# Expert weights loaded in rows of 8 KB through 16 ring places instead of rows of 4 KB through 32

## The chip, the cores and the metric

The kernel runs on one core of one Trainium2 chip. Its time is the device time of one execution in microseconds (us). Before the change the median of three runs was 1579.39 us (1577.28 to 1581.19). A separate execution was recorded by the hardware profiler; it took 1578.24 us, and its span, from the first to the last instruction, was 1576.4 us. The names of the engines are those of the profile: PE (matrix products), PEld (its weight loads), DVE, ACT, POOL, SP. SP's instructions here are almost only DMA issues; 16 DMA engines do the transfers.

## The reference

One layer of a decoder trunk over 512 tokens of width 1024, all in float32:

```python
u   = x @ w_in                                  # (512, 1024) @ (1024, D_IN_PROJ)
mix = concat[SSD(u_a), RWKV7(u_b), GLA(u_c), mLSTM(u_d)] @ w_out
x   = LayerNorm(DEEPNORM_ALPHA * x + mix)
h   = DEEPNORM_ALPHA * x + MoE(x)               # top 4 of 32 experts
h   = h + sigmoid(h @ ple_gate_w) * (p @ ple_proj)
x   = LayerNorm(h)

# MoE: for each token its 4 experts by router logits, gate = softmax of the 4
hg, hl = split(x @ w_gu[e] + b_gu[e])           # w_gu[e]: 1024 x 2048
hg, hl = min(hg, 7), clip(hl, -7, 7)
y      = ((hl + 1) * hg * sigmoid(1.702 * hg)) @ w_down[e] + b_down[e]   # w_down[e]: 1024 x 1024
```

RWKV7 is a recurrence over the tokens with a 64 x 64 state for each of 4 heads; the kernel computes it in blocks of tokens, one block after the other. The expert weights are 32 x 12 MB, by far most of what is read.

## The kernel before

The work has four stages. In the first, the four mixers are computed; in the second, the product with `w_out`, the first LayerNorm and the router, which ranks the experts and writes lists of each expert's tokens. The third is the MoE, the fourth the gate product with `ple_gate_w` and the second LayerNorm.

An expert's 12 MB are read as 24 units of 512 KB, each a tile of 128 partitions x 1024 floats, so that a row of a unit, what one partition receives, is 4 KB. Units 0 to 15 hold the gate and up weights (line 1297, tile `gu`), units 16 to 23 the down weights (line 1308, tile `dn`). The host stores the weights in this layout. The tokens of an expert are gathered from `x1d` by POOL (line 1208, `xg`), transposed by PE (line 1279, `tr`) and then multiplied in groups: 18 of the experts take three groups and 14 take two, 82 groups in all. Every group walks through the whole expert's weights, as four products of 128x512 for each 1024 rows of `gu`.

The units pass through a ring of places in SBUF, used in the fixed order `seq`. The places belong to pools that serve the mixers or the tail at other times:

```python
seq = ["rb"] * 7 + ["r2"] * RING2 + ["rb"] * (SLOTS["rb"] - 9) + ["wr"] * 2 + ["r3"] * RING3 + ["rb"] * 2
```

That is 32 places of 4 KB a partition, and four more (`pp`) that are used in the first round alone. `ahead` (line 898) issues 15 units while the out-projection runs (`"pf": {(0,1):15}`); the rest is issued by `unit`, for the first two experts from fixed addresses (line 1231), for the others from an address that SP reads from the router's result (line 1229). A place is given to a new unit when `used` has been called for the old one:

```python
if old is not None and not kept[old]:
    return False
w = R["raw"]()
...
sy.dma_start(w[:, None], A["we"][bass.ds(place[j], 1), u].rearrange("o p n -> p o n"))
```

The order of the instructions of one engine is set when the kernel is built, by a list scheduler that takes the next ready instruction by its own estimate of times; in the MoE PE's order is held to the order of the code. On the chip each engine runs its list in order, and a wait holds up all that stands behind it. SP's DMA loads wait for the place to be free and, as there are eight completion counters on its queue, for the load eight before it.

In the mixers, the 14 `rb` places hold RWKV's tiles: `sgw`, `aa`, `gg`, `rk`, `rr`, `kp` (elementwise inputs), `AR`, `KB` and `G` (operands and Gram blocks), `Lx` (the blocks to be inverted), `AQ` and `Tt` (the inverse and its pieces). The chain is: `G` products, a solve on DVE, `Q` and `Z` products (PE, `AQ`), then the sequential steps with `U<-W,Tt`, transposes `oT`, and `y_rwkvh`, `y_rwkvl`, which the out-projection (`mix`) reads. In between PE has the other mixers' input projections (`pj`, `pt`).

Of the kernel before, what the change touches and what calls it, by code (L numbers as in the profile page):

```python
# [8 lines left out]
F32 = mybir.dt.float32  # L9
# [11 lines left out]
D = 1024  # L21
E = 32
# [1 line left out]
KT = 8  # L24
C0 = math.exp(-0.5)

SLOTS = {"rb": 14, "xh": 8, "wr": 2, "wh": 2, "wl": 2, "zb": 4, "zc": 7, "yy": 2, "rc": 4, "rd": 6, "mc": 5, "md": 4}
BANKS = {"r": 2, "o": 1, "p": 2, "m": 3}
RING2 = 8
RING3, XG, AB = 8, 2, 2  # L30
NS = 3


BIG = 18
TURN = [0, 1] + sorted(range(2, 32), key=lambda r: (r - 1.5) / (BIG - 2) if r < BIG else (r - BIG + 0.7) / (32 - BIG))
GROUPS_OF = [NS if r < BIG else NS - 1 for r in range(32)]
OPT = {"conv": ("sx0",), "lnt": ("vv","va","aa","va"), "lov": ("zb",), "pl": (0,5,8,13,16,21), "pt": (), "em": 20, "wk": 6, "ml": 0, "hold": 0, "gm": (0,), "pe": 0, "order": "SABZDIgvLqmoM", "wm": (10,8,0), "bn": (), "ad": (), "rb": (2,0,3), "pf": {(0,1):15}, "ex": 4, "xq": 1, "aq": 1,  "ap": 2, "t1": (8,8), "pa": 1,  "op": ((2,1),(0,))}
EMPTY = 4096.0


# [86 lines left out]
def mixers(tc, nc, A, rbp, dram, mix, ctx, ident, ones, tri, x1d, accd, R, dbg):  # L127
# [153 lines left out]
    def rwkv():  # L281
# [103 lines left out]
        td = [dram.tile([2, 2, 32, 512], F32, name=f"td{n}") for n in range(2)]  # L385
        for t_, src in zip(td, (Tx, Tn)):
            sy.dma_start(t_.rearrange("q d b n -> (q d b) n"), flat(src))
        AQ = tl("rb", [128, 32, 32], "AQ")
        Tt = [tl("rb", [128, 16, 64], f"Tt{n}") for n in range(2)]
        for q in range(2):  # L390
            sy.dma_start(AQ[64 + 16 * q:80 + 16 * q], td[0][q, 0].rearrange("b (t u) -> t b u", u=32))
# [481 lines left out]
    def wout(h, kq, *tags):  # L873
        return split(A["wO"][h, kq], [128, 2, 512], "wo", *tags)

    seq = ["rb"] * 7 + ["r2"] * RING2 + ["rb"] * (SLOTS["rb"] - 9) + ["wr"] * 2 + ["r3"] * RING3 + ["rb"] * 2

    room = {**SLOTS, "r2": RING2, "r3": RING3, "pp": NT}

    def raw(look=False):  # L880

        n = R["n"]
        if n < len(seq) + OPT["ex"]:
            tag = (seq[:-2] + ["pp"] * OPT["ex"] + seq[-2:])[n]
        else:
            tag = seq[(n - OPT["ex"]) % len(seq)]
        if look:
            return tag, R["at"].get(tag, 0) % room[tag]
        R["n"] += 1
        R["at"][tag] = R["at"].get(tag, 0) + 1  # L890
        return R["pools"][tag].tile([128, D], F32, name="w", tag=tag, bufs=room[tag])

    def ahead(n):

        for _ in range(n):
            R["taken"].append(raw(look=True))
# [162 lines left out]
def moe(ctx, tc, nc, A, ident, rbp, R, x1d, accd, ovt, ove, out, dbg):  # L1059
# [64 lines left out]
    def gateweights():  # L1124

        for k in range(KT):
            w = ring[len(srcs) - KT + k]
            pool, tag, n = [(R["pools"]["r3"], "r3", RING3), (R["pools"]["wr"], "wr", SLOTS["wr"])][k] if k < 2 else (rbp, "rb", SLOTS["rb"])
            hi, lo = (pool.tile([128, D], F32R, name=x, tag=tag, bufs=n) for x in ("wh", "wl"))
            s.activation(hi, w, AF.Copy)  # L1130
            v.tensor_sub(lo, w, hi.bitcast(F32))
            wg.append((hi, lo))


    def ordered(m):
# [79 lines left out]
    def unit(tag_of, src):  # L1215

        if R["pre"]:
            ring.append(R["pre"].pop(0))
            return True
        tag, n = R["peek"]()  # L1220
        old = waits.get((tag, n))
# [3 lines that stand above are left out]
        if isinstance(src, tuple):  # L1225
            j, u = src
            if j not in place:
                place[j] = nc.values_load(eii[0:1, TURN[j]:TURN[j] + 1], engines=[mybir.EngineType.SP], min_val=0, max_val=E - 1)
            sy.dma_start(w[:, None], A["we"][bass.ds(place[j], 1), u].rearrange("o p n -> p o n"))
        else:  # L1230
            sy.dma_start(w, src)
        waits[tag, n] = len(ring)
        ring.append(w)
        return True

    srcs = []
    for e in range(E):
        if e == OPT["em"]:
            srcs += [A["pT"], A["pproj"][0], A["pproj"][1]]
        srcs += [A["we"][e, u] if e < 2 else (e, u) for u in range(24)]  # L1240
    srcs += [A["pgw"][k] for k in range(KT)]
    base = lambda e: 24 * e + (3 if e >= OPT["em"] else 0)
# [50 lines left out]
    def up(p, e, xT, g_, ks, last):  # L1293
        for k in ks:
            for c in range(4):
                w = ring[base(e) + 2 * k + c // 2][:, 512 * (c % 2):512 * (c % 2) + 512]
                ordered(pe.matmul(p[32 * c:32 * c + 32], xT[:, k, g_:32 * GROUPS_OF[TURN[e]]:GROUPS_OF[TURN[e]]], w,  # L1297
                                  start=False, stop=(k == KT - 1), tile_position=(0, 32 * c)))
            if last:
                used(base(e) + 2 * k)  # L1300
                used(base(e) + 2 * k + 1)

    def down(p, e, hT, ks, last):
        m = None
        for k in ks:
            for c in range(4):
                w = ring[base(e) + 16 + k][:, 256 * c:256 * c + 256]
                m = ordered(pe.matmul(p[32 * c:32 * c + 32, 0:256], hT[:, k % 2, 32 * (k // 2):32 * (k // 2) + 32], w,  # L1308
                                      start=False, stop=(k == KT - 1), tile_position=(0, 32 * c)))
            if last:  # L1310
                used(base(e) + 16 + k)
        return m

    def swiglu(p):
# [30 lines left out]

    def embed(i, tag):

        at = base(OPT["em"]) - 3
        pT, *pw = ring[at:at + 3]
        ppt.append(tp.tile([128, D], F32, name=f"pp{i}", tag="pp", bufs=NT))  # L1350
        tk = slice(128 * i, 128 * i + 128)
        for h in range(2):
            p = bank(tag, "emb")
            n = slice(512 * h, 512 * h + 512)
            for k in range(2):
                ordered(pe.matmul(p, pT[:, 512 * k:512 * k + 512][:, tk], pw[k][:, n], start=(k == 0), stop=(k == 1)))
            s.activation(ppt[i][:, n], p, AF.Copy)
        if i == NT - 1:
            for i in range(3):
                used(at + i)  # L1360

    def blocks():
# [35 lines left out]
    def overflow(then):  # L1398
        with tc.tile_pool(name="ov", bufs=1) as ov:
            n = nc.values_load(tot[0:1, 0:1], min_val=0, max_val=24)  # L1400
            with tc.For_i(0, n, 1) as j:
# [23 lines left out]
                v.scalar_tensor_tensor(gi_, d[:, 0:1], EMPTY, d[:, 1:2], op0=ALU.add, op1=ALU.add)  # L1425
                v.tensor_add(d[:, 3:4], d[:, 2:3], d[:, 3:4])
                v.tensor_add(d[:, 3:4], d[:, 3:4], d[:, 4:5])
                def big(name):
                    return ring2.tile([128, D], F32, name=name, tag="r2", bufs=RING2)

                x = big("x")
                g.memset(x, 0.0)
# [193 lines left out]
def _lay_out(inp, experts=True):  # L1626
# [77 lines left out]
```

## Time and profile before

| | |
|---|---|
| median of 3 runs | 1579.39 us (1577.28 to 1581.19) |
| profiled execution | 1578.24 us, span 1576.4 us |
| PE busy | 1462.9 us (93%) |
| PEld, DVE, ACT, POOL busy | 776.0, 522.9, 301.7, 218.2 us |
| DMA | 466.13 MB, 296 GB/s over the span |

The first `gu` product starts 404.64 us after the span's start. A product's busy time includes waits inside PE's pipeline, since the ends of products are modelled; so PE busy at 93% does not say that PE works at its peak for 93% of the span. In the rows below a window gives a stretch in us from the start of the span; the DMA share is that of 16 engines (it can be a little over 1, as the packets of several queues on one engine overlap in the record).

### The profile page before, as it was taken

Reading aid. Unit: us, or ns where it says so; the run is one execution under the profiler, and the core shown is the slowest. Engines: PE = TensorE matmul, PEld = TensorE weight load, DVE = VectorE, ACT = ScalarE, POOL = GpSimd, SP = SyncE. Lnnn points to the kernel's source line nnn. Section 1 sums busy time; section 2 is a strip of 40 time slices with the busy share of each in tenths; the row PEclk is TensorE's granted clock in tenths of the full one; section 3 lists DMA queues with packets and bytes.
Section 4 is the critical chain, followed back from the end, with each engine's and each line's share of the span. In section 5 each row is a group of like instructions: output and inputs, shape, how many; then the busy total and the mean of one; then the engine's idle time right before and its main releaser. Section 6 shows DMA issues by size and latency. Waiting matters only on the chain. (4 is left out here: it accounts for less than half of the span.)

```text
span 1576.4 us, 36036 instructions
## 1 busy us (share of the span) xinstructions
PE 1462.9 (93%) x14672; PEld 776.0 (49%) x14672; DVE 522.9 (33%) x1597; ACT 301.7 (19%) x632; POOL 218.2 (14%) x222
## 2 busy tenths in 40 slices
PE   9989999997799999999999999999999998999985
PEld 5769879886244433443334333334434343334364
DVE  5688875668521112111121111111121111111155
ACT  4343523523011111110111110101111110111120
POOL 1011211003011211211111111111111211111100
PEclk9899999997899999999999999999999999999998
DMA  4222311654979999999999999999999999999931
GB/s 165 61 67 64 113 44 52 235 224 159 346 275 366 360 387 393 380 390 379 381 384 382 369 380 376 383 382 378 335 389 388 379 387 373 390 380 392 390 104 42
DMA packets 148012, 466.13 MB, mean 296 GB/s; under 512 B 27121, under 2 KB 36162, under 8 KB 147810
## 3 DMA queue, kind: packets, MB, share of 16 engines
q1 hardware_dynamic: 131666, 442.08, 74.2%
q0 software_dynamic: 14992, 18.90, 5.8%
q8 instruction: 117, 1.92, 0.5%
q10 hardware_dynamic: 1184, 2.80, 0.5%
q14 instruction: 53, 0.43, 0.1%
HBM read 452.08 MB, written 18.43 MB: 298 GB/s over the span
## 5 line engine op out<-in xcount | busy, mean ns | idle before, releaser
L1297 PE MATMUL gu<-w,x 128*32 128x512 f32 x5248 | 627.4, 596 | 22.7 <-DMA w<-in_we_dram 21.7
L1297 PEld LDWEIGHTS gu<-w,x 128*32 128x32 f32 x5248 | 189.1, 119 | 442.6 <-issue 292.8
L1316 DVE TENSOR_SCALAR a<-gu 128x256 f32<-128x256 f32 x82 | 34.8, 425 | 895.8 <-PE gu L1297 895.8
L1308 PE MATMUL dn<-w,h 128*32 128x256 f32 x5248 | 304.0, 387 | 0.6 <-issue 0.6
L1308 PEld LDWEIGHTS dn<-w,h 128*32 128x32 f32 x5248 | 160.4, 112 | 121.0 <-issue 8.7
L1327 POOL DMA_INDIRECT accd<-y,ixs x82 | 128.0, 1561 | 357.9 <-ACT y L1326 330.2
L1317 ACT ACTIVATE c<-a 128x256 f32<-128x256 f32 x82 | 34.2, 417 | 631.7 <-DVE a L1316 630.1
L1208 POOL DMA_INDIRECT xg<-x1d,ixt x32 | 32.8, 1025 | 585.2 <-PE tr L1279 524.1
L1326 ACT ACTIVATE y<-dn,gate 128x256 f32<-128x256 f32 x82 | 36.7, 473 | 273.2 <-PE dn L1308 273.2
L1279 PE MATMUL tr<-ident,xg 96*128 96x96 f32 (+1 forms) x256 | 31.6, 251 | 31.3 <-ACT h L1267 18.1
L1279 PEld LDWEIGHTS tr<-ident,xg 96*128 96x128 f32 (+1 forms) x256 | 22.6, 142 | 42.3 <-ACT h L1267 24.8
L158 DVE TENSOR_TENSOR wl<-w,wh 128x1024 fp32r<-128x1024 f32 x28 | 34.2, 1220 | 15.0 <-ACT wh L157 14.9
L1320 DVE TENSOR_TENSOR b<-b,c 128x256 f32<-128x256 f32 x82 | 34.9, 425 | 5.4
L1264 PE MATMUL tr<-ident,b 128*128 128x128 f32 x164 | 32.3, 298 | 4.7 <-DVE b L1320 1.6
L1319 DVE SCALAR_TENSOR_TENSOR b<-b,a 128x256 f32<-128x256 f32 x82 | 34.5, 421 | 1.8
L157 ACT ACTIVATE wh<-w 128x1024 fp32r<-128x1024 f32 x28 | 29.5, 1053 | 25.6 <-PE pj L144 17.4
L1280 ACT ACTIVATE x<-tr 128x384 f32<-128x384 f32 (+1 forms) x64 | 27.7, 443 | 34.2 <-PE tr L1279 33.2
L1318 DVE TENSOR_SCALAR b<-gu 128x256 f32<-128x256 f32 x82 | 34.0, 415 | 0.0
L1267 ACT ACTIVATE h<-tr 128x256 f32<-128x256 f32 x82 | 29.4, 381 | 15.1 <-PE tr L1264 12.2
L1089 DVE TENSOR_SCALAR pt<-iotas,rankm 128x384 bf16<-128x384 bf16 (+1 forms) x132 | 30.9, 295 | 0.0
L1289 PEld LDWEIGHTS <-sel 96*32 96x32 bf16 x656 | 17.8, 98 | 21.7 <-issue 9.9
L1596 PE MATMUL gu<-wh,hh 128*128 128x512 f32 (+1 forms) x72 | 27.6, 387 | 0.3 <-ACT hh L1554 0.3
(650 smaller groups left out, 1683.5 us busy)
## 6 DMA issues: line engine op xcount, KB each, us to landing
w<-in_we_dram SPq DMA_DIRECT2D x768, 512.0 KB
w<-in_wA_dram SPq DMA_DIRECT2D x18, 512.0 KB
w<-in_wT_dram SPq DMA_DIRECT2D x10, 512.0 KB
wo<-in_wO_dram SPq DMA_DIRECT2D x8, 512.0 KB
w<-in_pgw_dram SPq DMA_DIRECT2D x8, 512.0 KB
x<-in_xT_dram SPq DMA_DIRECT2D x4, 512.0 KB
xt<-in_xt_dram SPq DMA_DIRECT2D x4, 512.0 KB
x1d<-xt ACTq DMA_DIRECT2D x4, 512.0 KB
```

What stands on the lines that cost most here:

```text
L158: v.tensor_sub(wl, w, wh.bitcast(F32))
L1208: return g.indirect_dma_start(out=xg[TURN.index(e) % XG][0:n], out_offset=None, in_=x1d, in_offset=bass.IndirectOffsetOnAxis(ap=ixt[0:n, e ...
L1279: ordered(pe.transpose(p[:, n * k:n * k + n], xg[j % XG][0:n, c:c + 128], ident[0:n, 0:n]))
L1297: ordered(pe.matmul(p[32 * c:32 * c + 32], xT[:, k, g_:32 * GROUPS_OF[TURN[e]]:GROUPS_OF[TURN[e]]], w, start=False, stop=(k == KT - 1), ti ...
L1308: m = ordered(pe.matmul(p[32 * c:32 * c + 32, 0:256], hT[:, k % 2, 32 * (k // 2):32 * (k // 2) + 32], w, start=False, stop=(k == KT - 1), ...
L1316: v.tensor_scalar(a, p[:, 0:256], 7.0, None, op0=ALU.min)
L1317: s.activation(c, a, AF.Sigmoid, scale=1.702)
L1318: v.tensor_scalar(b, p[:, 256:512], 7.0, -7.0, op0=ALU.min, op1=ALU.max)
L1319: v.scalar_tensor_tensor(b, b, 1.0, a, op0=ALU.add, op1=ALU.mult)
L1320: v.tensor_mul(b, b, c)
L1326: last = s.activation(y, p[:, 0:256], AF.Copy, scale=gate[:, r, s_:s_ + 1]).ins
L1327: x = g.indirect_dma_start(out=accq, out_offset=bass.IndirectOffsetOnAxis(ap=ixs[:, r, s_:s_ + 1], axis=0), in_=y, in_offset=None, compute ...
```

## The change

Two units become one transfer of 1 MB with rows of 8 KB, and two neighbouring places of the ring become one of 8 KB a partition. The host interleaves each two units. SBUF space stays as it is.

- `SLOTS["rb"]` goes from 14 to 4. Ten places become five tiles of 8 KB (`PAIRS`), allocated once at the start of the mixers; a table `HALF` gives each of RWKV's and some other mixer tiles a fixed half, and where a half serves several tiles they follow each other in a fixed order. `AQ` is written over `Lx`.
- `r2` and `r3` go from 8 tiles of 4 KB to 4 of 8 KB, `pp` from four to two.
- `wr` (one ring place) and `rb` (two) remain pools of 4 KB tiles: such a place is a list of two tiles and is loaded by two DMAs of 512 KB. So 13 of the 16 places take one DMA with rows of 8 KB, and 3 take two with rows of 4 KB.
- Ahead of the MoE six places (12 old units) are loaded instead of 15 units.
- In the MoE `used` is called once for both halves. The tail's gate weights and hidden tiles are halves of 8 KB tiles, in the same way.

```diff
-SLOTS = {"rb": 14, "xh": 8, "wr": 2, ...
+SLOTS = {"rb": 4, "xh": 8, "wr": 2, ...
-RING2 = 8
-RING3, XG, AB = 8, 2, 2
+RING2 = 4
+RING3, XG, AB = 4, 2, 2
+PAIRS = 5
+HALF = {"sgw": 0, "aa": 1, "gg": 2, "rk": 3, "rr": 4, "ep": 5, "em": 6, "kp": 7, "AR0": 8, "AR1": 9, "G1": 3, "G2": 0,
+        "G3": 1, "rv": 6, "Tt0": 5, "Tt1": 7, "mq": 3, "mk": 5, "z_mo": 0}
-... "pf": {(0,1):15}, "ex": 4, ...
+... "pf": {(0,1):6}, "ex": 2, ...
@@ mixers
+    R["pairs"] = [rbp.tile([128, 2 * D], F32, name=f"pair{i}", tag="pair", bufs=PAIRS) for i in range(PAIRS)]
+
     def tl(tag, shape, name, dtype=F32):
+        if name in HALF:
+            n = HALF[name]
+            t = R["pairs"][n // 2][:, D * (n % 2):D * (n % 2) + D]
...
-        AQ = tl("rb", [128, 32, 32], "AQ")
+        AQ = Lx
@@ ring
-    seq = ["rb"] * 7 + ["r2"] * RING2 + ["rb"] * (SLOTS["rb"] - 9) + ["wr"] * 2 + ["r3"] * RING3 + ["rb"] * 2
-    room = {**SLOTS, "r2": RING2, "r3": RING3, "pp": NT}
+    seq = [3, 4] + ["r2"] * RING2 + [0, 1, 2] + ["wr"] + ["r3"] * RING3 + ["rb"] * 2
+    room = {**{i: 1 for i in range(PAIRS)}, "r2": RING2, "r3": RING3, "pp": NT // 2, "wr": 1, "rb": 2}
...
-        return R["pools"][tag].tile([128, D], F32, name="w", tag=tag, bufs=room[tag])
+        if tag in ("wr", "rb"):
+            return [R["pools"][tag].tile([128, D], F32, name="w", tag=tag, bufs=SLOTS[tag]) for _ in range(2)]
+        if tag in range(PAIRS):
+            return R["pairs"][tag]
+        return R["pools"][tag].tile([128, 2 * D], F32, name="w", tag=tag, bufs=room[tag])
+
+    def loaded(w, src):
+        if isinstance(w, list):
+            for h in range(src.shape[-1] // D):
+                sy.dma_start(w[h], src[:, D * h:D * h + D])
+        else:
+            sy.dma_start(w[:, 0:src.shape[-1]], src)
...
@@ up, down
-                w = ring[base(e) + 2 * k + c // 2][:, 512 * (c % 2):512 * (c % 2) + 512]
+                w = part(base(e) + k, 512 * c, 512)
...
-                used(base(e) + 2 * k)
-                used(base(e) + 2 * k + 1)
+                used(base(e) + k)
...
-                w = ring[base(e) + 16 + k][:, 256 * c:256 * c + 256]
+                w = part(base(e) + 8 + k // 2, D * (k % 2) + 256 * c, 256)
...
-            if last:
-                used(base(e) + 16 + k)
+            if last and k % 2:
+                used(base(e) + 8 + k // 2)
@@ host layout
+    def pairs(z):
+        z = z.reshape(*z.shape[:-3], z.shape[-3] // 2, 2, 128, D)
+        return np.swapaxes(z, -3, -2).reshape(*z.shape[:-3], 128, 2 * D)
...
-        r["we"] = np.concatenate([gu, a["exp_w_down"][0].reshape(E, KT, 128, D)], 1)
+        r["we"] = pairs(np.concatenate([gu, a["exp_w_down"][0].reshape(E, KT, 128, D)], 1))
```

The order of instructions moves with it, as the scheduler sees other tiles. On SP, from the out-projection to the router's result, the loads stood so before (`wo` is the out-projection's weight, `w` an expert unit, `bias` and `rw` the experts' biases and the router's weight):

```order
L155 DMA wo<-in_wO_dram 128x1024 x3
L898 DMA w<-in_we_dram 128x1024 x8
L1025 DMA bias<-biasd 96x3072
L155 DMA wo<-in_wO_dram 128x1024 x3
L898 DMA w<-in_we_dram 128x1024 x7
L1231 DMA w<-in_we_dram 128x1024 x4
L837 DMA rw<-in_rw_dram 128x256
L1231 DMA w<-in_we_dram 128x1024 x17
```

The same place of SP's list after the change (`pair_...` is one of the five tiles; 128x2048 is 1 MB):

```order
L166 DMA wo<-in_wO_dram 128x1024 x2
L914 DMA pair_111<-in_we_dram 128x2048
L914 DMA pair_110<-in_we_dram 128x2048
L166 DMA wo<-in_wO_dram 128x1024
L914 DMA w<-in_we_dram 128x2048 x4
L1050 DMA bias<-biasd 96x3072
L166 DMA wo<-in_wO_dram 128x1024 x2
L912 DMA w<-in_we_dram 128x1024 x2
L166 DMA wo<-in_wO_dram 128x1024
L912 DMA w<-in_we_dram 128x1024 x2
L848 DMA rw<-in_rw_dram 128x256
```

The two first places are now tiles of the mixers, and their loads stand between two loads of `wo`. On PE, RWKV's `Q` products stood so among the projections before:

```order
L144 MATMUL pt<-wl,x0h 128x256 x2
L144 MATMUL pt<-wl,x1h 128x256 x2
L144 MATMUL Q<-AQ,G_450 32x32 x8
L144 MATMUL Q<-AQ,G_451 32x32 x8
L263 MATMUL yT<-ident,ys 128x128 x2
```

and so after, with `Lx` for `AQ`:

```order
L155 MATMUL pj<-x1h,wl 128x512 x2
L155 MATMUL pj<-x2h,wl 128x512
L155 MATMUL Q<-Lx,G_445 32x32 x8
L155 MATMUL Q<-Lx,pair_108 32x32 x8
L274 MATMUL yT<-ident,ys 128x128 x2
L155 MATMUL pj<-x2h,wl 128x512
L155 MATMUL pj<-x3h,wl 128x512 x2
```

Counted from the start of PE's list, the first `Q` stands behind 288 `pj` and 156 `pt` products before, and behind 325 and 288 after: 37 and 132 more. PE's list in the MoE is the same but for names.

## Rows read from the trace of the kernel before

**Rows 1.** The page: span, and the loads' queue (packets, MB, share of 16 engines).

```profile
span 1576.4 us, 36036 instructions
...
q1 hardware_dynamic: 131666, 442.08, 74.2%
```

**Rows 2.** Windows by stage; columns as in the first line.

```profile
core 0: us, PE busy (x) PEld busy (x) DVE busy (x) ACT busy (x) POOL busy (x), PEclk, DMA share, GB/s
0.00:404.00 404.00, 367.07 (x2338) 306.05 (x2342) 295.95 (x792) 154.50 (x290) 58.63 (x109) 0.91 0.38 127
...
740.00:1494.00 754.00, 712.49 (x8128) 290.48 (x8124) 113.88 (x436) 88.37 (x217) 104.30 (x74) 1.00 1.03 381
```

**Rows 3.** Windows of line 1297 (`gu`) alone: PE busy, PEld busy, clock, DMA share, GB/s.

```profile
446.00:740.00 294.00, 167.98 (x1546) 51.22 (x1548) 0.98 1.02 375
740.00:1494.00 754.00, 436.65 (x3512) 131.14 (x3508) 1.00 1.03 381
```

**Rows 4.** Waits of SP's queue, 446 to 1494 us: total, times, longest.

```profile
SPq L1229 <- DMA w<-in_we_dram: 564.7, 624, 5.8
SPq L1229 <- PE gu L1297: 49.6, 95, 5.7
```

**Rows 5.** DMA, 446 to 1494 us.

```profile
DMA packets 118719, 397.30 MB, mean 379 GB/s; under 512 B 15996, under 2 KB 24065, under 8 KB 118594
...
q1 hardware_dynamic: 104274, 379.73, 94.1%
...
w<-in_we_dram SPq DMA_DIRECT2D x716, 512.0 KB
w<-in_pgw_dram SPq DMA_DIRECT2D x8, 512.0 KB
```

**Rows 6.** DMA, 744 to 745 us, where q1 alone is active.

```profile
DMA packets 110, 0.41 MB, mean 406 GB/s; under 512 B 11, under 2 KB 11, under 8 KB 110
...
q1 hardware_dynamic: 110, 0.41, 99.6%
```

**Rows 7.** DMA, 489.2 to 489.4 us, with one 8 KB packet on q14.

```profile
q1 hardware_dynamic: 24, 0.08, 102.5%
q14 instruction: 1, 0.01, 9.7%
```

**Rows 8.** The page's row of q8.

```profile
q8 instruction: 117, 1.92, 0.5%
```

**Rows 9.** DMA, 146 to 148 us, with small packets alone.

```profile
q1 hardware_dynamic: 1506, 0.09, 49.9%
```

**Rows 10.** Waits of SP's queue, 446 to 520 us.

```profile
SPq L1229 <- PE gu L1297: 26.6, 14, 5.7
SPq L1229 <- PE dn L1308: 18.1, 14, 5.5
```

**Rows 11.** Timeline, 388 to 405 us: start, us, engine, line [idle before <- releaser].

```profile
391.56 3.78 SPq L1231 DMA_DIRECT2D w<-in_we_dram  x8
...
394.00 1.20 POOL L1208 DMA_INDIRECT xg<-x1d,ixt  x1 [1.83 <-DVE key L1161]
...
401.94 1.51 PE L1279 MATMUL tr<-ident,xg 96*128 96x96 f32 x8 [8.61 <-DMA xg<-x1d,ixt]
...
404.64 1.07 PE L1297 MATMUL gu<-w,x 128*32 128x512 f32 x4
```

**Rows 12.** Windows of the `pj` products up to 404 us.

```profile
0.00:404.00 404.00, 110.38 (x432) 84.15 (x432) 23.95 (x33) 12.97 (x19) 0.91 0.38 127
```

**Rows 13.** Windows of the `pt` products up to 404 us.

```profile
0.00:404.00 404.00, 69.63 (x484) 62.88 (x484) 4.32 (x12) 7.58 (x20) 0.91 0.38 127
```

**Rows 14.** Timeline of PE: RWKV's steps (first, third, fourth, last) and the product that follows.

```profile
160.40 0.50 PE L144 MATMUL U<-W,Tt 64*64 64x64 f32 x5
...
208.13 0.44 PE L144 MATMUL U<-W,Tt 64*64 64x64 f32 x4
...
216.30 0.38 PE L144 MATMUL U<-W,Tt 64*64 64x64 f32 x3
...
285.62 0.44 PE L144 MATMUL U<-W,Tt 64*64 64x64 f32 x4
...
306.33 0.48 PE L144 MATMUL mix<-woh,y_rwkvh 128*128 128x512 f32 x1
```

More of the change, by code (lines that the diff above doesn't have):

```diff
@@ L25 @@
 C0 = math.exp(-0.5)
-SLOTS = {"rb": 14, "xh": 8, "wr": 2, "wh": 2, "wl": 2, "zb": 4, "zc": 7, "yy": 2, "rc": 4, "rd": 6, "mc": 5, "md": 4}
+SLOTS = {"rb": 4, "xh": 8, "wr": 2, "wh": 2, "wl": 2, "zb": 4, "zc": 7, "yy": 2, "rc": 4, "rd": 6, "mc": 5, "md": 4}
 BANKS = {"r": 2, "o": 1, "p": 2, "m": 3}
-RING2 = 8
-RING3, XG, AB = 8, 2, 2
+RING2 = 4
+RING3, XG, AB = 4, 2, 2
 NS = 3
@@ L36 @@
 GROUPS_OF = [NS if r < BIG else NS - 1 for r in range(32)]
-OPT = {"conv": ("sx0",), "lnt": ("vv","va","aa","va"), "lov": ("zb",), "pl": (0,5,8,13,16,21), "pt": (), "em": 20, "wk": 6, "ml": 0, "hold": 0, "gm": (0,), "pe": 0, "order": "SABZDIgvLqmoM", "wm": (10,8,0), "bn": (), "ad": (), "rb": (2,0,3), "pf": {(0,1):15}, "ex": 4, "xq": 1, "aq": 1,  "ap": 2, "t1": (8,8), "pa": 1,  "op": ((2,1),(0,))}
+PAIRS = 5
+HALF = {"sgw": 0, "aa": 1, "gg": 2, "rk": 3, "rr": 4, "ep": 5, "em": 6, "kp": 7, "AR0": 8, "AR1": 9, "G1": 3, "G2": 0,
+        "G3": 1, "rv": 6, "Tt0": 5, "Tt1": 7, "mq": 3, "mk": 5, "z_mo": 0}
+OPT = {"conv": ("sx0",), "lnt": ("vv","va","aa","va"), "lov": ("zb",), "pl": (0,5,8,13,16,21), "pt": (), "em": 20, "wk": 6, "ml": 0, "hold": 0, "gm": (0,), "pe": 0, "order": "SABZDIgvLqmoM", "wm": (10,8,0), "bn": (), "ad": (), "rb": (2,0,3), "pf": {(0,1):6}, "ex": 2, "xq": 1, "aq": 1,  "ap": 2, "t1": (8,8), "pa": 1,  "op": ((2,1),(0,))}
 EMPTY = 4096.0
@@ L135, in mixers @@
     pg = mix.enter_context(tc.tile_pool(name="pg", bufs=1, space=PSUM))
+    R["pairs"] = [rbp.tile([128, 2 * D], F32, name=f"pair{i}", tag="pair", bufs=PAIRS) for i in range(PAIRS)]
     def tl(tag, shape, name, dtype=F32):
+        if name in HALF:
+            n = HALF[name]
+            t = R["pairs"][n // 2][:, D * (n % 2):D * (n % 2) + D]
+            names = "abcd"[:len(shape) - 1]
+            return t.rearrange(f"p ({' '.join(names)}) -> p {' '.join(names)}", **dict(zip(names, shape[1:])))
         return {"rb": rbp, "zb": wz, "zc": wz, "rd": wz, "wr": wrp, "yy": wq, "rc": wq, "mc": wq}.get(tag, wk).tile(shape, dtype, name=name, tag=tag, bufs=SLOTS[tag])
@@ L890, in raw @@
         R["at"][tag] = R["at"].get(tag, 0) + 1
-        return R["pools"][tag].tile([128, D], F32, name="w", tag=tag, bufs=room[tag])
+        if tag in ("wr", "rb"):
[9 more added lines that the diff above has]
+            sy.dma_start(w[:, 0:src.shape[-1]], src)
+    R["loaded"] = loaded
     def ahead(n):
@@ L897, in ahead @@
             w = raw()
-            sy.dma_start(w, A["we"][0, len(R["pre"])])
+            loaded(w, A["we"][0, len(R["pre"])])
             R["pre"].append(w)
@@ L1126, in gateweights @@
         for k in range(KT):
-            w = ring[len(srcs) - KT + k]
-            pool, tag, n = [(R["pools"]["r3"], "r3", RING3), (R["pools"]["wr"], "wr", SLOTS["wr"])][k] if k < 2 else (rbp, "rb", SLOTS["rb"])
-            hi, lo = (pool.tile([128, D], F32R, name=x, tag=tag, bufs=n) for x in ("wh", "wl"))
+            w = part(len(srcs) - KT // 2 + k // 2, D * (k % 2), D)
+            if k in (0, KT - 2, KT - 1):
+                q = "rb" if k else "wr"
+                hi, lo = (R["pools"][q].tile([128, D], F32R, name=x, tag=q, bufs=SLOTS[q]) for x in ("wh", "wl"))
+            else:
+                t = rbp.tile([128, 2 * D], F32R, name="whl", tag="pair", bufs=PAIRS)
+                hi, lo = t[:, 0:D], t[:, D:2 * D]
             s.activation(hi, w, AF.Copy)
@@ L1228, in unit @@
                 place[j] = nc.values_load(eii[0:1, TURN[j]:TURN[j] + 1], engines=[mybir.EngineType.SP], min_val=0, max_val=E - 1)
-            sy.dma_start(w[:, None], A["we"][bass.ds(place[j], 1), u].rearrange("o p n -> p o n"))
-        else:
-            sy.dma_start(w, src)
+            src = A["we"][bass.ds(place[j], 1), u].rearrange("o p n -> p (o n)")
+        R["loaded"](w, src)
         waits[tag, n] = len(ring)
@@ L1238, in moe, with part @@
         if e == OPT["em"]:
[L1239 to L1242, printed above, removed]
+            srcs += [A["pT"], A["pproj"]]
+        srcs += [A["we"][e, u] if e < 2 else (e, u) for u in range(12)]
+    srcs += [A["pgw"][k] for k in range(KT // 2)]
+    base = lambda e: 12 * e + (2 if e >= OPT["em"] else 0)
+    def part(i, at, n):
+        w = ring[i]
+        return w[at // D][:, at % D:at % D + n] if isinstance(w, list) else w[:, at:at + n]
     npre = len(R["pre"])
@@ L1346, in embed @@
     def embed(i, tag):
[L1348 to L1351, printed above, removed]
+        at = base(OPT["em"]) - 2
+        if i % 2 == 0:
+            t = tp.tile([128, 2 * D], F32, name=f"pp{i}", tag="pp", bufs=NT // 2)
+            ppt.extend((t[:, 0:D], t[:, D:2 * D]))
         for h in range(2):
@@ L1355, in embed @@
             for k in range(2):
-                ordered(pe.matmul(p, pT[:, 512 * k:512 * k + 512][:, tk], pw[k][:, n], start=(k == 0), stop=(k == 1)))
+                ordered(pe.matmul(p, part(at, 512 * k + 128 * i, 128), part(at + 1, D * k + 512 * h, 512), start=(k == 0), stop=(k == 1)))
             s.activation(ppt[i][:, n], p, AF.Copy)
         if i == NT - 1:
-            for i in range(3):
+            for i in range(2):
                 used(at + i)
@@ L1427, in overflow @@
                 v.tensor_add(d[:, 3:4], d[:, 3:4], d[:, 4:5])
+                half = {}
                 def big(name):
-                    return ring2.tile([128, D], F32, name=name, tag="r2", bufs=RING2)
+                    if name in half:
+                        return half.pop(name)[:, D:2 * D]
+                    t = ring2.tile([128, 2 * D], F32, name=name, tag="r2", bufs=RING2)
+                    if name in ("x", "act"):
+                        half[{"x": "xT", "act": "hT"}[name]] = t
+                    return t[:, 0:D]
                 x = big("x")
@@ L1449, in product @@
                         wt = big("wt")
-                        sy.dma_start(wt[:, None], A["we"][bass.ds(e, 1), units[k]].rearrange("o p n -> p o n"))
+                        sy.dma_start(wt, A["we"][bass.ds(e, 1), units[k] // 2][:, :, D * (units[k] % 2):][:, :, 0:D].rearrange("o p n -> p (o n)"))
                         for i in range(2):
@@ L1546, in transposed @@
     def transposed(src):
-        hi, lo = (r3.tile([128, KT, 128], F32R, name="h" + x, tag="r3", bufs=RING3) for x in "hl")
+        t = r3.tile([128, 2, KT, 128], F32R, name="hhl", tag="r3", bufs=RING3)
+        hi, lo = t[:, 0], t[:, 1]
         for h in range(2):
@@ L1571, in finish @@
         for i in range(NT):
-            hs.append(ring2.tile([128, D], F32, name=f"h{i}", tag="r2", bufs=RING2))
+            if i % 2 == 0:
+                t = ring2.tile([128, 2 * D], F32, name=f"h{i}", tag="r2", bufs=RING2)
+                hs += [t[:, 0:D], t[:, D:2 * D]]
             for n in (slice(0, 512), slice(512, D)):
@@ L1673, in _lay_out @@
     r["bias"] = np.concatenate([bg, a["exp_b_down"][0]], 1)
+    def pairs(z):
+        z = z.reshape(*z.shape[:-3], z.shape[-3] // 2, 2, 128, D)
+        return np.swapaxes(z, -3, -2).reshape(*z.shape[:-3], 128, 2 * D)
     if experts:
         gu = a["exp_w_gu"][0].reshape(E, KT, 128, 2, 2, 2, 256).transpose(0, 1, 4, 2, 5, 3, 6).reshape(E, 16, 128, D)
-        r["we"] = np.concatenate([gu, a["exp_w_down"][0].reshape(E, KT, 128, D)], 1)
+        r["we"] = pairs(np.concatenate([gu, a["exp_w_down"][0].reshape(E, KT, 128, D)], 1))
     r["pT"] = a["p"][0, 0].T.reshape(2, 128, T).transpose(1, 0, 2).reshape(128, 2 * T)
-    r["pproj"] = a["ple_proj"][0].reshape(2, 128, D)
-    r["pgw"] = a["ple_gate_w"][0].reshape(KT, 128, D)
+    r["pproj"] = pairs(a["ple_proj"][0].reshape(2, 128, D))[0]
+    r["pgw"] = pairs(a["ple_gate_w"][0].reshape(KT, 128, D))
     return {k: np.ascontiguousarray(v) for k, v in r.items()}
```

## The prediction

> **What bounds the kernel now.** I read first the page's head, then the windows by stage, then the windows of the `gu` products alone, then what SP waits for, and last the DMA view down to single packets.
>
> The span is 1576.4 us, and the loads' queue q1 keeps the 16 DMA engines at work for 74.2% of it [rows 1]. That mean hides two kinds of stage [rows 2]: up to 404 us PE works 367.07 of 404 us and the DMA share is 0.38 (bound by PE and RWKV's chain); from 740 to 1494 us the DMA share is 1.03, at 381 GB/s. There PE looks busy too (712.49 of 754 us), so the reader must see that part of it is waiting. The `gu` products come in fours that share the array: from 446 to 740 us 167.98 us for 1546, or 434.6 ns a four; after 740 us 436.65 us for 3512, or 497.3 ns [rows 3]. The work is the same, so 878 fours x 62.7 ns = 55 us of PE's busy time is waiting for weights that have not landed. Idle time for the same reason comes on top and is left out. SP agrees: it waits 564.7 us in 624 waits for the load eight before, and 49.6 us for `gu` to free a place [rows 4]. From 740 us on the loads set the pace, and PE has at least 55 us to give: loads that are faster by less than that shorten the kernel by what they gain.
>
> **Part 1: rows of 8 KB for 4 KB.** From 446 to 1494 us 716 units are loaded [rows 5]; a unit has 128 rows, 8 for each DMA engine, so an engine moves 5728 rows of 4 KB. With 13 of 16 places on 8 KB, 4654 of them become 2327. The price of a 4 KB row: in the microsecond 744 to 745 q1 has 110 packets at 99.6% [rows 6]; 11 are under 512 B, and at 10.6 ns each (part 2) they take 0.12 us; (0.996 x 16 - 0.12) / 99 = 160 ns. The loads of before show no 8 KB row. The nearest is one 8 KB packet of another queue under full load: 9.7% of 16 x 0.2 us = 310 ns [rows 7]. So two rows become one that is 2 x 160 - 310 = 10 ns cheaper, and 2327 x 10 = **23.3 us** go.
>
> The bounds. Over 446 to 1494 us a 4 KB packet takes a little more: 94.1% of 16 x 1048 us, less 11,600 small ones at 10.6 ns, over 92,700 large ones (379.73 MB / 4 KB), is 169 ns [rows 5]. Against that a row of 310 to 322 ns saves 16 to 28 ns, and the upper half of that is what a crowd of queues adds to any packet; I bound with 16 ns, or -37 us. On the other side the row of q8 speaks: 117 packets with 16 KB each take 0.5% of 16 x 1576.4 us, or 1.08 us each [rows 8], 66 ns per KB against 39 for a 4 KB row. By it large rows would gain nothing, or lose. I take the 8 KB packet, since it has the size in question and ran in the middle of the same loads, and keep zero as the other end.
>
> [...]
>
> The `pgw` loads (8 x 8 rows an engine, [rows 5]) become pairs too: -0.3 us.
>
> **Part 2: completions.** Each load ends with one small packet on each engine. From 146 to 148 us small packets stand alone: 1506 at 49.9% of 16 x 2 us, 10.6 ns each [rows 9]. The 716 loads become 716 x (3/16 + 13/32) = 425; 291 x 10.6 ns = -3 us.
>
> **Part 3: coarser places.** A place comes free when both halves are used, and is usable when 1 MB has landed. That costs where the ring is full and SP waits for PE: 446 to 520 us, 26.6 + 18.1 = 44.7 us [rows 10]. The loads that start late there are missed later, when the transfers set the pace. A unit takes 512 KB / 379 GB/s = 1.4 us. I take one for the place held longer and one and a half for loads not started in that stretch: +3.4 us. Bounds: nothing (the ring is as large as before, 36 units in the first round), and the whole of those 44.7 us once more at a tenth, 5 us. When the ring runs empty, after 740 us, coarser places cost no rate: eight loads are then outstanding as before, and they hold 8 MB instead of 4 MB.
>
> **Part 4: the first gather.** At 391.56 us eight loads are issued; `xg` starts at 394.00, and PE waits 8.61 us for it until 401.94, before the first `gu` at 404.64 [rows 11]. This is on the path. Its packets share the engines with the loads. With 96 rows of 4 KB there are 6 for an engine; if each waits behind one 8 KB row instead of a 4 KB row, that is 6 x (310 - 160) = 0.9 us, and the writing of `x1d` ahead of it has as many: **+1.5 us** (0 to 4).
>
> **Part 5: the mixers.** No arithmetic is added, but halves with a fixed order and the new sizes change the scheduler's order. RWKV's first `Q` now stands behind 37 `pj` and 132 `pt` products more. At 110.38 us / 432 = 256 ns [rows 12] and 69.63 / 484 = 144 ns [rows 13] that is 9.5 + 19.0 = 28.5 us of PE work. It is moved, not added, and PE has it to do anyway; it costs only where the chain behind it cannot be shortened. Before, the chain's first step is at 160.40 us and its eighth at 285.62, 17.9 us a step [rows 14]; PE fills the time between. Starting at 189 the same end needs 13.8 us a step; the fastest step of before, from 208.13 to 216.30, takes 8.2 us [rows 14]. So the chain can make it up, with less work left to fill the last steps: **+2 us** (-3, if the new order fits better, to the 28 us of rival C).
>
> **What costs nothing.** 12 units instead of 15 are prefetched in the out-projection; the first `gu` doesn't read weights before 404 us, and eight loads issued at 391.56 [rows 11] show that the ring is being filled until then, with or without the three. If that cover were gone, three units would cost 4.2 us. SP issues 40% fewer loads; it was waiting anyway. The two first places stand between two `wo` loads in SP's list, and wait for RWKV's last reads of their tiles; `wo` stood behind eight such places before. `AQ` over `Lx`, the tail's halves and the overflow path have the same instructions.
>
> **Sum.** -23.3 - 0.3 - 3 + 3.4 + 1.5 + 2 = -19.7 us, all against the profiled execution of 1578.24 us: 1558.5. That execution lies 1.15 us under the median of the runs, 1579.39, so on the scale of the runs it is 1559.7; I say **1559 us**.
>
> **The rivals.**
>
> A, the forecast: transfers in the MoE get about 2 to 4% faster and PE's waiting shrinks by as much. Own range: part 1 between 12 and 37 us, the rest +/- 5: 1543 to 1572.
>
> B, the rows cost nothing less. What limits 381 GB/s is then behind the engines (memory, or the way into SBUF), or the loads are cut into 4 KB packets whatever their row: the change does not do what it says. For it: the rate is flat in the whole stage [rows 2], and q8's row. Against it: in rows 6 the engines reach 406 GB/s for a microsecond, so 381 is no hard limit. Without part 1 and its completions: 1578.24 + 3.4 + 1.5 + 2 = 1585, with completions 1582; taken as 1583. [...]
>
> C, slower: RWKV's chain does not make up the 28.5 us. PE takes its list in order, so when the steps need more than 13.8 us each, PE stands at the products with `y_rwkvh` (306.33 us before, rows 14), and out-projection, router and MoE start later by up to 28 us; the loads cannot use that time, as the ring is full. Time: 1578.24 - 19.7 + 28 = 1587. For it: the mean step was 17.9 us. Against it: PE was busy through those steps, so 17.9 us is what was put between them, and the fastest is 8.2.
>
> D, half of it: the overhead that a row sheds is about 5 ns, as it would be if the 8 KB packet of rows 7 profited from an idle moment of its queue, or if the ring of 16 coarse places runs dry at the change from expert to expert. -23.3 becomes -8 to -12: 1572 to 1575. [...]
>
> **How the numbers follow.** A 0.65, D 0.12, B 0.12, C 0.09, others 0.02. Within 0.3%, about what a measurement of this kernel can tell from no change, is 1574.7 to 1584.1. Faster: all of A, nearly all of D, 0.76. Same: most of B and a rest of D, 0.13. Slower: C, a part of B, 0.11. The range goes from A's lower end, 1543, to B's time, 1583; it leaves out C and the tails.
>
> **What would show it.** Right: q1's packets fall from 131666 to about 87,000 with the same MB; the rate from 740 us on rises from 381 to about 390 GB/s; fours of `gu` there fall from 497 to about 475 ns; the first `gu` starts between 404 and 410 us. Wrong in part 1: packets nearly halved, and the rate still 381 (B), or packets not halved. Wrong in part 5: the first `gu` after 420 us with a wait of PE at `mix` <- `y_rwkvh` (C). Wrong in part 3: SP's waits for `gu` and `dn` grow by more than 30 us after 520 us.

## The result, and the profile after

The changed kernel takes 1561.38 us (median of 4 runs, 1559.67 to 1564.6) against 1578.34 us before (4 runs): a ratio of 0.9886, with a 95% interval of 0.9869 to 0.9902. That is 17 us; forecast were 20.4. The profiled execution took 1559.67 us. Every ratio here leaves out runs over 1.5% above the fastest of their kernel, which only the run with loads of 64 partitions had.

The page of the kernel after, its span and the loads' queue, beside [rows 1]:

```profile
span 1557.9 us, 34852 instructions
...
q1 hardware_dynamic: 85874, 442.05, 73.1%
```

The same bytes now go in 85,874 packets instead of 131,666 (forecast: about 87,000). The windows of after, by stage, answer to [rows 2] (busy time of each engine, granted clock, DMA share, GB/s); the second fence is line 1331, the `gu` products, as in [rows 3]:

```profile
0.00:404.00 404.00, 363.36 (x2346) 300.43 (x2350) 295.94 (x798) 155.16 (x291) 63.96 (x109) 0.92 0.38 128
...
740.00:1478.00 738.00, 678.58 (x8088) 273.65 (x8081) 113.90 (x436) 88.55 (x216) 104.29 (x74) 0.99 1.01 387
```

```profile
740.00:1478.00 738.00, 402.74 (x3480) 114.41 (x3469) 0.99 1.01 387
```

The rate of the long stage rose from 381 to 387 GB/s (forecast 390), and a four of `gu` fell from 497 to 402.74 / 870 = 463 ns (forecast 475). This second sign is no measure of the row length: with loads of 1 MB in rows of 4 KB (an experiment below, 11 us slower) a four takes 398.62 / 865 = 461 ns.

```profile
740.00:1478.00 738.00, 398.62 (x3460) 112.61 (x3460) 0.98 1.02 382
```

That the loads still set the pace is read from SP's waits, shown further down.

The MoE begins with the first `gu` and ends with the last `y`. The timeline of before has the end at 1493.93 us:

```profile
1493.93 0.90 ACT L1326 ACTIVATE y<-dn,gate 128x256 f32<-128x256 f32 x2 [6.47 <-PE dn L1308]
```

The timeline of after, from the router's `rank` to the last `y`:

```profile
387.35 0.18 PE L1072 MATMUL rank<-mskb,trib 128*128 128x32 bf16 x1 [5.21 <-DVE mskb L1006]
...
391.11 1.20 POOL L1237 DMA_INDIRECT xg<-x1d,ixt  x1 [1.16 <-DVE key L1190]
...
400.71 1.51 PE L1313 MATMUL tr<-ident,xg 96*128 96x96 f32 x8 [10.27 <-DMA xg<-x1d,ixt]
...
403.40 6.93 PE L1331 MATMUL gu<-pair,x 128*32 128x512 f32 x48
...
1478.41 0.91 ACT L1359 ACTIVATE y<-dn,gate 128x256 f32<-128x256 f32 x2 [6.47 <-PE dn L1341]
```

With [rows 11] the MoE took 1493.93 - 404.64 = 1089.3 us before and 1478.41 - 403.40 = 1075.0 after: 14.3 of the 18.5 us that the span lost. The rest, 1.2 us before the MoE and 3 us behind it, is within what one kernel varies: a second profile of the changed kernel, below, has its first `gu` 2.2 us later and 81.5 us instead of 79.5 behind the last `y`. Forecast for the MoE were 23.2 us, so 9 are missing. The windows of after show a pause of the transfers that takes part of them:

```profile
740.00:1085.00 345.00, 318.30 (x3784) 128.29 (x3773) 54.56 (x214) 41.53 (x101) 50.61 (x36) 0.99 1.02 392
1085.00:1120.00 35.00, 34.25 (x345) 14.20 (x348) 4.44 (x19) 6.15 (x13) 4.12 (x3) 1.00 0.75 270
1120.00:1465.00 345.00, 314.62 (x3812) 126.13 (x3808) 51.69 (x195) 39.38 (x98) 49.56 (x35) 1.00 1.02 395
```

and those of before, with the same pause, shallower:

```profile
740.00:1100.00 360.00, 340.21 (x3836) 135.77 (x3836) 54.52 (x214) 41.93 (x102) 50.61 (x36) 1.00 1.03 380
1100.00:1135.00 35.00, 34.45 (x344) 14.28 (x340) 4.43 (x19) 5.55 (x12) 4.12 (x3) 1.00 0.91 325
1135.00:1480.00 345.00, 325.81 (x3796) 135.25 (x3787) 51.73 (x195) 39.33 (x98) 49.57 (x35) 1.00 1.03 386
```

For 35 us around expert 20 the transfers slow down. Against the rate ahead of it this pause costs (392 - 270) x 35 = 4.3 MB, or 10.9 us, after, and (380 - 325) x 35 = 1.9 MB, or 5.1 us, before. That is 5.8 us more after; the experiments show that less than this reaches the end. SP's waits from 520 us on point to a cause (total, times, longest):

```profile
SPq L914 <- DMA w<-in_we_dram: 376.2, 212, 4.3
SPq L912 <- DMA pair<-in_we_dram: 141.0, 61, 4.3
SPq L914 <- DMA pair<-in_we_dram: 87.5, 40, 3.1
SPq L912 <- DMA w<-in_we_dram: 75.5, 58, 2.9
SPq L914 <- PE gu L1331: 21.1, 41, 1.7
SPq L914 <- PE dn L1341: 20.0, 20, 6.6
SPq L912 <- PE emb L1389: 16.5, 2, 16.2
SPq L912 <- PE gu L1331: 4.9, 14, 1.0
...
SPq L912 <- PE dn L1341: 3.0, 8, 0.7
```

SP waits 680 us for earlier loads and 49 us for `gu` and `dn` to free a place, so the loads still set the pace. In one wait of 16.2 us SP stands before a place that still holds an operand of `emb`. Before, SP waited 2.8 us in all for `emb`. (`emb` is the product that makes the per-layer embedding term `p @ ple_proj` of the reference.) The embedding's `pT` and `pproj` arrive ahead of expert 20's weights and are used in four parts, the last behind that expert's `dn` products. Eight loads are outstanding: in the trace SP's loads take eight semaphores in turn, and in the 229 cases from 740 to 1478 us that have the landing of the eighth load before on record, a load starts 0.016 us or more behind it, 0.118 us in the median. Since the change they are eight of 16 places instead of eight of 36 or 32, up to 8 MB instead of 4 MB, so SP comes round to the held place while expert 20's own weights are still landing.

### The profile page after: what moved, and what is told of

The parts are those of the page before. It is cut to its first block, busy times and chain, and to the rows that moved or that the text cites. A ratio compares the mean times of both kernels' runs of the same rounds, so it can differ in the third digit from the quotient of the medians.

```text
span 1557.9 us, 34852 instructions
## 1 busy us (share of the span) xinstructions
PE 1425.1 (91%) x14671; PEld 752.9 (48%) x14672; DVE 520.0 (33%) x1597; ACT 301.2 (19%) x632; POOL 223.6 (14%) x222
## 3 DMA queue, kind: packets, MB, share of 16 engines
q1 hardware_dynamic: 85874, 442.05, 73.1%
## 5 line engine op out<-in xcount | busy, mean ns | idle before, releaser
L1331 PE MATMUL gu<-w,x 128*32 128x512 f32 x3568 | 418.0, 599 | 30.8 <-DMA w<-in_we_dram 29.9
L1331 PEld LDWEIGHTS gu<-w,x 128*32 128x32 f32 x3568 | 119.8, 119 | 309.4 <-issue 215.4
L1341 PE MATMUL dn<-w,h 128*32 128x256 f32 x3664 | 211.4, 383 | 0.0
L1331 PE MATMUL gu<-pair,x 128*32 128x512 f32 x1680 | 196.0, 598 | 9.5 <-DMA pair<-in_we_dram 9.4
L1341 PEld LDWEIGHTS dn<-w,h 128*32 128x32 f32 x3664 | 110.9, 111 | 82.7 <-issue 2.7
L1331 PEld LDWEIGHTS gu<-pair,x 128*32 128x32 f32 x1680 | 55.3, 119 | 135.8 <-issue 103.2
L1341 PE MATMUL dn<-pair,h 128*32 128x256 f32 x1584 | 94.7, 389 | 1.1 <-DMA pair<-in_we_dram 1.1
L1341 PEld LDWEIGHTS dn<-pair,h 128*32 128x32 f32 x1584 | 48.2, 112 | 37.8 <-issue 3.2
```

## The experiments

In each the theory was written first; the comparison is with the kernel before on the same chip.

**The embedding at once.** All four parts stand at the start of expert 20.

```diff
         if j == OPT["em"]:
-            embed(0, "dn")
+            for i in range(NT):
+                embed(i, "dn")
...
-            if j == OPT["em"] and k == 3:
-                embed(1, "dn")
...
-        if j == OPT["em"]:
-            embed(2, "dn")
...
-        if j == OPT["em"]:
-            embed(3, "gu")
```

> The changed kernel with all four parts of the PLE embedding at the start of expert 20, instead of spread to the end of its down products; nothing else. Theory (part of the gain is given back there: the places of pT and pproj stay held until the last part, and with 8 MB instead of 4 MB of loads outstanding SP reaches them early): SP's wait of 16.5 us for emb falls under 4 us, the rate over the 35 us around it rises from 270 to over 350 GB/s, time 1554 to 1558 us against 1561.4. Rival (the dip is PE's 14.8 us of emb products, during which no weights are used): the dip stays, only in one piece, 1560 to 1564 us.

Measured: 1558.04 us, ratio 0.9872 (0.9842 to 0.9901). SP waits for `emb` no more, and the pause is gone; the windows of this run:

```profile
1060.00:1130.00 70.00, 69.21 (x718) 28.69 (x722) 5.33 (x25) 10.51 (x22) 9.81 (x7) 0.98 1.02 389
1130.00:1460.00 330.00, 307.51 (x3736) 126.70 (x3728) 51.55 (x195) 39.41 (x98) 49.56 (x35) 0.98 1.02 390
```

So the held places made the pause, not PE's embedding products, which are the same here. Behind that point the rate is 390 GB/s, not the 395 of the kernel with the pause. The intervals of the two kernels' ratios overlap, so they are measured side by side below.

**Two loads with rows of 4 KB for each place.** Places, order and mixers of the changed kernel; only the loads of the experts' weights are as before.

```diff
+        if len(src.shape) == 3:
+            for h in range(2):
+                sy.dma_start(w[h] if isinstance(w, list) else w[:, D * h:D * h + D], src[h])
...
-        r["we"] = pairs(np.concatenate([gu, a["exp_w_down"][0].reshape(E, KT, 128, D)], 1))
+        r["we"] = np.concatenate([gu, a["exp_w_down"][0].reshape(E, KT, 128, D)], 1).reshape(E, 12, 2, 128, D)
```

> The changed kernel with expert weights in the old layout: each place of 8 KB is filled by two loads of 512 KB with rows of 4 KB. Places, order and mixers as in the changed kernel. Theory (the row length makes the rate): q1 has about 131,000 packets again, the rate in the middle of the MoE falls from 392 to about 380 GB/s, the dip at the embedding shrinks since 4 MB are outstanding again, time 1576 to 1584 us. Rival (places, order or mixers made the gain): 1559 to 1565 us. The first gather lands earlier by about 1.5 us than with 8 KB rows.

Measured: 1577.48 us (10 runs, 1571.42 to 1582.2), ratio 0.9995 (0.9981 to 1.0010). With the old loads nothing is left of the gain: new places, coarser release and reordered mixers together cost or bring -0.8 us, with an interval from -3.0 to 1.6. The profiled execution was the fastest of the ten, so its rates are on the high side. The pause shrank, as expected. From 1060 to 1130 us, in this run, the next one (loads of 1 MB again) and the changed kernel:

```profile
1060.00:1130.00 70.00, 68.61 (x718) 28.95 (x714) 9.95 (x41) 12.21 (x27) 9.81 (x7) 1.00 0.94 346
```

```profile
1060.00:1130.00 70.00, 67.19 (x710) 28.09 (x710) 7.95 (x36) 11.50 (x25) 9.82 (x7) 1.00 0.90 329
```

```profile
1060.00:1130.00 70.00, 67.99 (x708) 27.40 (x704) 5.02 (x21) 9.48 (x21) 9.29 (x7) 1.00 0.89 332
```

Against the 381, 386 and 392 GB/s of 740 to 1040 us that is 2.5, 4.0 and 4.2 MB lost; the kernel before loses 1.9 MB in its pause. SP's wait for `emb` is shorter than the 16.5 us of the changed kernel too:

```profile
SPq L912 <- PE emb L1392: 11.7, 3, 10.9
```

So by these runs the depth of the pause follows the bytes outstanding, 4 or 8 MB, and hardly the new places.

**One load of 1 MB with rows of 4 KB.** The same data, fetched for both halves by one DMA.

```diff
+                sy.dma_start(w.rearrange("p (h n) -> p h n", h=2), src.rearrange("h p n -> p h n"))
```

> As the run with two loads, but one load of 1 MB with rows of 4 KB for each place of 8 KB. Theory (row length): the rate stays at 380 to 384 GB/s in the middle of the MoE, and the dip at the embedding is as deep as in the changed kernel, time 1578 to 1588 us. Rival (fewer loads and completions made the gain): rate 390 GB/s or more, 1559 to 1565 us.

Measured: 1572.18 us (10 runs, 1570.45 to 1575.52), ratio 0.9958 (0.9946 to 0.9970). Neither side was right. 41% fewer loads with the same rows bring 0.37%, 5.8 us by the ratios; the means of the two sets of ten runs on this chip differ by 5.0 us, with an interval from 2.7 to 7.3. The row length brings the rest: from 0.9958 to 0.9886, 11.4 us, or, with the 0.9900 of a second measurement below, 9.2 us; each is sure to some 3 us. This run's profile puts 239 us of SP's waits from 520 us on down to `gu` and `dn`, where the changed kernel has 49, but they are no waits for a place: when PE ends an expert after 740 us, SP has issued 12 to 19 units beyond it (5 at the pause) of the ring's 32, about as in the changed kernel. The windows from 740 to 1040 us, with two loads, one load with 4 KB rows, and the changed kernel:

```profile
740.00:1040.00 300.00, 283.74 (x3270) 112.80 (x3270) 48.38 (x191) 35.27 (x87) 43.72 (x32) 0.98 1.03 381
```

```profile
740.00:1040.00 300.00, 272.26 (x3290) 110.46 (x3290) 48.38 (x191) 35.25 (x87) 44.96 (x32) 0.98 1.03 386
```

```profile
740.00:1040.00 300.00, 274.18 (x3322) 110.76 (x3315) 48.41 (x191) 35.34 (x87) 44.92 (x32) 0.98 1.02 392
```

and the loads' queue in the same 300 us (packets, MB, share of 16 engines), in the same order:

```profile
q1 hardware_dynamic: 29944, 109.03, 94.6%
```

```profile
q1 hardware_dynamic: 29006, 110.62, 95.0%
```

```profile
q1 hardware_dynamic: 18312, 112.36, 94.2%
```

Share x 16 x 300 us / MB is 41.6, 41.2 and 40.2 us of an engine for a MB. The step by row length, 2.4%, is 8 ns on a pair of rows (2 x 4 KB at 41.2 us a MB, 338 ns), taken over all pairs; as only 13 of 16 places have long rows, it is 10 ns for each pair that became one row, as forecast. But the queue's MB rose by 1.6% only, in three more profiles with rows of 8 KB by 1.2 to 1.4%: 5 to 7 ns for such a pair. The difference lies in records that overlap. The 16 engines have more than 16 packets of q1 on record at once for 23% of these 300 us with one load in 4 KB rows, and for 13% in the changed kernel; so it is not only packets of several queues that overlap. A merged pair is 10 ns shorter in the record, and the stream gains 5 to 7 by it.

**The embedding at once, in the kernel before.** The same four edits.

> The kernel before with all four parts of the embedding at the start of expert 20; nothing else. Theory (held places stop the loads there too, but less with 4 MB outstanding): the rate over the 35 us around it rises from 325 to over 360 GB/s, time 1573 to 1577 us against 1578.3. Rival (the dip is PE's): 1577 to 1581 us.

Measured: 1577.83 us, ratio 0.9995 (0.9980 to 1.0010). The pause is gone there too (378 GB/s from 1060 to 1130 us), as the theory has it, and the time did not move, against the theory; it is in the range of the rival. Behind it the rate is 381 GB/s, where the kernel with the pause has 386.

**Two loads with rows of 8 KB.** Each load of 1 MB cut by partitions, to have the old number of loads with the new rows.

```diff
-            sy.dma_start(w[:, 0:src.shape[-1]], src)
+            for h in range(2):
+                sy.dma_start(w[64 * h:64 * h + 64, 0:src.shape[-1]], src[64 * h:64 * h + 64])
```

> The changed kernel with each load of 1 MB cut into two of 512 KB by partitions (64 and 64): rows of 8 KB as in the changed kernel, number of loads as with two loads of 4 KB rows. From 200 to 640 us after the first gu those two kernels load 391 and 381.5 GB/s, and the one with one load of 4 KB rows 385.7. Theory (two effects that add: row length +1.4%, half as many loads +1.1%): 386 to 388 GB/s there, time 1565 to 1573 us, and the pause at the embedding shorter than in the changed kernel since 4 MB are outstanding. Rival (rows alone, the gain of one load with 4 KB rows came from elsewhere): 390 GB/s or more, 1558 to 1563 us. Rival (number of loads alone): 381 to 383 GB/s, 1575 us or more.

Measured: 2208.87 and 2235.96 us in the two runs that the ratio of 1.4088 (1.4017 to 1.4159) rests on; five more took 2287 to 2360 us, and the profile is of one of them, at 2346.06 us. No expectation came near. It does not tell the theories apart, as it changed something else: which partitions one load writes. From 900 to 1200 us (its windows, then its queue q1):

```profile
900.00:1200.00 300.00, 196.78 (x1910) 73.38 (x1906) 27.46 (x107) 19.94 (x49) 25.30 (x18) 0.88 1.02 220
```

```profile
q1 hardware_dynamic: 10884, 62.82, 95.3%
```

By the record the 16 engines are as busy as in the changed kernel (DMA share 1.02, q1 at 95.3% against 94.2%) and move 220 GB/s, 209 of it on q1: 72.8 us of an engine for a MB, where the changed kernel has 40.2. A load of this run writes 64 partitions instead of 128, but no run varied the partitions alone, so why the rate fell was not shown. What rows of 8 KB bring with the old number of loads stays open.

**The changed kernel and the embedding at once, side by side.** No new edits.

> The changed kernel once more, for a comparison on one chip with the next run: 1559 to 1564 us. The first gu again at 403 us, the tail from the last dn to the end 79 to 82 us.

> The changed kernel with the embedding at the start of expert 20, once more beside the changed kernel. Theory (the pause of the transfers there costs the end 4 to 5 units, some 6 us): 4 to 7 us below the changed kernel. Rival (the pause is given back later by faster rows, as the row durations after it suggest): within 2 us of it.

Measured: the changed kernel 1561.69 us, ratio 0.9900 (0.9883 to 0.9918); with the embedding at once 1558.52 us, 0.9879 (0.9865 to 0.9894), 3.2 us less, between the two expectations. The intervals overlap, but the slowest of its four runs (1559.25) lies under the fastest of the changed kernel's (1559.61), and the first measurements of the two differ by 3.3 us as well. This version is the fastest of all. The windows of the first, then of the second:

```profile
1085.00:1120.00 35.00, 34.20 (x324) 14.28 (x326) 4.43 (x19) 6.75 (x14) 4.12 (x3) 1.00 0.76 271
1120.00:1465.00 345.00, 319.70 (x3836) 127.76 (x3828) 51.74 (x195) 39.45 (x98) 49.57 (x35) 0.99 1.02 396
```

```profile
1085.00:1120.00 35.00, 34.23 (x386) 13.25 (x388) 4.43 (x19) 4.48 (x10) 4.12 (x3) 1.00 1.00 382
1120.00:1465.00 345.00, 321.41 (x3852) 128.16 (x3844) 52.56 (x198) 39.65 (x99) 49.58 (x35) 0.98 1.02 390
```

Without the pause (382 - 271) x 35 = 3.9 MB more arrive by 1120 us; in the next 345 us the other kernel catches up (396 - 390) x 345 = 2.1 MB. About half stays, 1.8 MB or 4.6 us at 390 GB/s; the runs show 3.2.

In this second profile of the changed kernel the timeline has `rank` at 389.65 us and the first `gu` at 405.62, where 403 was expected:

```profile
389.65 0.18 PE L1072 MATMUL rank<-mskb,trib 128*128 128x32 bf16 x1 [5.22 <-DVE mskb L1006]
...
405.62 2.77 PE L1331 MATMUL gu<-pair,x 128*32 128x512 f32 x12
```

The first profile had 387.35 and 403.40 for the same program, so stages before the MoE can be compared to some 2 us only.

## Why the prediction came out

**What binds: right.** The transfers set the pace from 740 us on, and what they gained came through to the time.

**Part 1, rows: right in kind, half in size.** Forecast 23.3 us, by runs 9 to 11 (from one load with 4 KB rows to the changed kernel). The packets' own durations bore out the 10 ns for a merged pair. The step that failed is the next one: that all of these 10 ns, 2327 times, leave the time. The records overlap, so that by the queue's rate 5 to 7 ns of the 10 are gained, and 11.4 us / 2327 = 4.9 ns reach the end, 4.0 with 9.2 us. That is the size which case D assumed, but not its reason, as the 8 KB packet of [rows 7], 310 ns, was no lucky one: from 740 to 1040 us those of the changed kernel take 313 ns in the median and 326 in the mean. The lower end of D's range, 8 us or 3.4 ns for a merged pair, is shown by no run; the runs show 9.2 to 11.4 us, 4.0 to 4.9 ns.

**Part 2, completions: forecast 3 us, by runs 5 to 6.** The interval begins at 2.7, so the runs alone do not exclude the forecast. The records say that a load costs the engines more than its last packets: 41.6 - 41.2 = 0.4 us a MB, where 12 small packets fewer at 10.6 ns are 0.1. The bytes outstanding doubled along with it, and with them the pause deepened (from 2.5 to 4.0 MB lost); these effects were not taken apart.

**Part 3, coarser places: the right size in the wrong place, by luck.** In the stretch where the ring is full no loss shows: 351 and 350 GB/s from 446 to 520 us in two profiles before, 347 to 358 in four after. From 520 us on SP's waits for `gu` and `dn` to free a place rose from 37 to 49 us, less than the 30 us that were to show the part wrong. Before they were:

```profile
SPq L1229 <- PE gu L1297: 23.1, 81, 1.6
SPq L1229 <- PE dn L1308: 13.8, 40, 1.7
```

What I had said to cost nothing, eight outstanding loads that "hold 8 MB instead of 4 MB", is one half of what cost something: the other is a place held long, at expert 20. Forecast +3.4 us, shown +3.2 by taking the pause away; the numbers agree, the mechanisms do not.

**Part 4, first gather: not settled.** From the issue of `xg` to `tr` 394.00 to 401.94, 7.9 us, before [rows 11]; 391.11 to 400.71, 9.6 us, after. In four profiles with rows of 8 KB it was 9.2 to 9.6, in the four with 4 KB 7.9 to 9.2, so the +1.5 us may be right, but the ranges touch. The start of the MoE says more: with the same order of instructions the two runs with 4 KB rows have the first `gu` at

```profile
400.73 5.82 PE L1334 MATMUL gu<-pair,x 128*32 128x512 f32 x48
```

```profile
401.48 5.86 PE L1337 MATMUL gu<-pair,x 128*32 128x512 f32 x48
```

and the four with 8 KB rows at 403.4 to 405.9. Most of that lies ahead of `xg`. Long rows may so cost 2 to 5 us there, more than forecast; with two profiles against four this is not shown.

**Part 5, mixers: right.** `Q` starts 16.8 us later (145.95 against 162.70), the first step `U` at 179.27 instead of 160.40, the last run of them about where it was, and `mix` finds `y_rwkvh` 0.7 us later than in [rows 14]. The timeline of after:

```profile
162.70 0.69 PE L155 MATMUL Q<-Lx,G 32*32 32x32 f32 x16
...
179.27 0.50 PE L155 MATMUL U<-W,pair 64*64 64x64 f32 x5
...
286.90 0.68 PE L155 MATMUL U<-W,pair 64*64 64x64 f32 x8
...
307.07 0.51 PE L155 MATMUL mix<-woh,y_rwkvh 128*128 128x512 f32 x1
```

The chain made it up, so C did not come. With the old loads the new order costs nothing that the runs can tell (0.9995): parts 3 and 5, forecast at 5.4 us together, are there within -3.0 to 1.6.

So the total was near, 17 us for 20.4, in part by luck, because errors offset each other: rows brought 12 to 14 us less than forecast, loads 2 to 3 more, and of the 7 us of costs beside the transfers the 5.4 of parts 3 and 5 do not show. The 1.5 of the gather, if it is there, is already taken off what the rows brought. The pause's 3.2 us is no further cost in this sum, as it is in what the larger loads brought.

## What to carry to other kernels

Where transfers set the pace, as here, look for two gains in fewer and larger loads, by row length (here 9.2 to 11.4 us) and by number of loads (here 5.0 to 5.8 us); a load of the same size with short rows tells the two apart. Test a sign before trusting it: the shorter `gu` products came with either row length (a four of 463 ns with 8 KB, 461 ns with 4 KB). Price a packet by the rate that a stage reaches and not only by the packet's record, as records overlap: a merged pair was worth 10 ns by the record and 5 to 7 by the rate. When loads grow and their number outstanding stays, look for every ring place that is held long: the issue position comes to it sooner, and one such place held the stream up here for 16 us.

## What the hardware showed that was not expected

With loads to 64 partitions the 16 engines were as busy (a DMA share of 1.02 in both), and the rate was 220 GB/s instead of 392. On q1 alone more packets than engines were on record at once for 13 to 23% of 300 us, and the durations overstated what a merged pair brought: 10 ns, against 5 to 7 by the rate. After the pause of the transfers at expert 20 the rate was higher for some 350 us than without it (396 against 390 GB/s, and 386 against 381 in the kernel before), so the pause was repaid in part, in the kernel before wholly; the cause is open.
